# Four MLPs on one core: the place of a few inner-activation tiles in the on-chip memory

## The chip, the cores and the metric

One core of a Trainium2 chip runs the whole program in one launch. The metric is the device time of that launch in microseconds; the kernel before takes 1617.34 us (median of three runs, 1616.33 to 1620.15).

## What is computed

An encoder of four layers over one sequence of 256 tokens with 1024 channels, all in fp32. A layer is a mixer and an MLP, each added to the residual x. The mixers are a bidirectional state-space mixer (layers 0 and 3), a dilated attention (layer 1) and a differential attention (layer 2). The change is in the MLP:

```
def sqrelu_mlp(h, w1, w2):                  # w1: 1024 x 4096, w2: 4096 x 1024
    return jnp.square(jax.nn.relu(h @ w1)) @ w2
x = x + sqrelu_mlp(rmsnorm(x, norm_mlp_g[i]), mlp_w1[i], mlp_w2[i])
```

## The kernel before, in words

All activations stand transposed: 128 channels of a block on the partitions, the 256 tokens along a row. A product in fp32 is made of three matmuls in the type float32r (`mm3`, L145 to L151): the weight's rounded part times the activation's rounded part (L149), the same weight times the activation's remainder (L150), and the weight's remainder times the activation's rounded part (L151). In `mm3` the weights are the stationary operand (`lhsT`, 128x128, 512 bytes of each partition) and the activations the moving one (`rhs`, 128x256, 1024 bytes of each partition), so every matmul has its own weight load.

**Weights.** They come as chunks of 512 KB into `raw` tiles (SyncE's queue, five buffers); ScalarE copies each to `whi` (L110), VectorE makes `wlo` (L112), five buffers of each. `pump` keeps a fixed number of chunks converted ahead of their use and of transfers ahead of the conversion.

**One MLP** (`mlp`) has eight slices s of 512 inner channels. `up(s)` takes 4 chunks and makes 96 matmuls: 8 blocks of the normalised input (the tiles `spl`) by 4 blocks of inner channels by 3. `evac(s, b)` makes relu, the norm's factor and the square on VectorE and ScalarE (L349, L351), then the rounded part `hh` and the remainder `hl` (L353, L354), in two halves of two row blocks each; a tile holds four row blocks j of 128 inner channels. `down(s)` takes 4 chunks, one for each j, and makes 96 matmuls: 4 row blocks by 8 output blocks by 3. The order is `up(0)`, `up(1)`, `down(0)`, `up(2)`, `down(1)`, ... `up(7)`, `down(6)`, `down(7)`. In the first MLP alone, `bias_vectors` (its matmuls are L721 and L722) stands between `up(2)` and `down(1)`, and `bias_rows` (transfers only) between `up(3)` and `down(2)`. The last `down` finishes the output blocks one by one (`proj_tail`), and the next part's squares and split tiles follow behind each.

**Places.** The built program gives each tile a fixed address in a partition. The weight tiles begin at 52,512 bytes and are 4096 bytes long, all of them at 288 modulo 512. The tiles `spl`, `hh`, `hl`, and the mixers' `nh` and `nl` all begin at 480 modulo 512, so that each moving operand of these lies 192 bytes past the weights' offset. Weight columns and tokens are stepped by whole multiples of 512 bytes, so the offset is the same for every matmul of a pair of tiles. Other pairs differ: in the differential attention the moving keys `k` and `kl` and the stationary queries `q` (`mm2`, L130 and L131) all begin at 0 modulo 512, a distance of 0; in the dilated attention `k` of L149 to L151 lies at a distance of 480 from `q` for part of the heads; `oh` and `tab` of L721 and L722 both lie at 480, a distance of 0. The pool `lp` of one part (an MLP or a mixer) is given back at its end, and the next part's pool begins at the same address, 127,456.

Of the kernel before, what the change touches and what calls it, by code (L numbers as in the profile page):

```python
# [10 lines left out]
F32 = mybir.dt.float32  # L11
F32R = mybir.dt.float32r
I32 = mybir.dt.int32
AF = mybir.ActivationFunctionType
ALU = mybir.AluOpType
PSUM = bass.MemoryType.PSUM
P = 128
T = 256
# [27 lines left out]
class Prog:  # L46
# [278 lines left out]
    def mlp(self, l, finish):  # L325
        nc = self.nc
        hs = {}
        acc = [self.bank(f"a{i}") for i in range(4)]

        def up(s):  # L330
            b = [self.bank(f"r{2 * (s % 2) + i}") for i in range(2)]
            for j in range(4):
                wh, wl = self.take(("up", l, s, j))
                for kk in range(2):
                    k = 2 * j + kk
                    for n in range(4):
                        c = slice(kk * 512 + n * P, kk * 512 + (n + 1) * P)
                        self.mm3(b[n // 2][:, (n % 2) * T:(n % 2 + 1) * T], wh[:, c], wl[:, c],
                                 self.uh[k], self.ul[k], k == 0 and n % 2 == 0, k == 7)
                self.done()  # L340
            return b

        def evac(s, b):
            hh = self.lp.tile([P, 4, T], F32R, tag="hh", name="hh", bufs=2)
            hl = self.lp.tile([P, 4, T], F32R, tag="hl", name="hl", bufs=2)
            for i in range(2):
                v = self.lp.tile([P, 2, T], F32, tag="v", name="v", bufs=3)
                sq = self.lp.tile([P, 2, T], F32, tag="vsq", name="vsq", bufs=2)
                nc.vector.scalar_tensor_tensor(out=v, in0=b[i].rearrange("p (n t) -> p n t", n=2), scalar=0.0,  # L349
                                               in1=self.rbc.unsqueeze(1).to_broadcast([P, 2, T]), op0=ALU.max, op1=ALU.mult)  # L350
                nc.scalar.activation(out=sq, in_=v, func=AF.Square)  # L351
                h = hh[:, 2 * i:2 * i + 2, :]
                nc.scalar.copy(out=h, in_=sq)  # L353
                nc.vector.tensor_tensor(out=hl[:, 2 * i:2 * i + 2, :], in0=sq, in1=h.bitcast(F32), op=ALU.subtract)  # L354
            hs[s] = (hh, hl)

        def down(s):
            hh, hl = hs.pop(s)
            if s < 7:
                for j in range(4):  # L360
                    wh, wl = self.take(("dn", l, s, j))
                    for n in range(8):
                        c = slice(n * P, (n + 1) * P)
                        self.mm3(acc[n % 4][:, (n // 4) * T:(n // 4 + 1) * T], wh[:, c], wl[:, c], hh[:, j, :], hl[:, j, :],
                                 s == 0 and j == 0 and n < 4, False)
                    self.done()
            else:
                self.proj_tail(acc, ("dn", l), [(hh[:, j, :], hl[:, j, :]) for j in range(4)], finish)

        b = up(0)  # L370
        self.norm_finish("a3")
        evac(0, b)
        for s in range(1, 8):
            b = up(s)
            evac(s, b)
            if s == 2 and not self.bvec:
                self.bias_vectors()
            if s == 3 and not self.rep:
                self.bias_rows()
            down(s - 1)  # L380
        down(7)

    def tail_chunks(self, key, w, k0, nk):
# [888 lines left out]
```

## Time and profile before

| what | us |
|---|---|
| median of three runs | 1617.34 |
| the profiled execution | 1616.8 |
| span of its trace (first to last instruction) | 1615.0 |
| TensorE (PE) busy | 1579.2 (98%) |
| VectorE (DVE) busy | 1193.0 (74%) |
| ScalarE (ACT) busy | 959.2 (59%) |
| transfers (DMA), mean | 186 GB/s |

The MLPs lie at about 262 to 432, 731 to 902, 1030 to 1197 and 1436 to 1607 us of the span. How to read the rows further on: a matmul's duration (0.28 us) covers its way through the pipeline, and the next one starts long before it ends; the pace is the distance from one start to the next. A row of a window counts the matmuls that touch it, some two or three more than begin in it.

### The profile page before, as it was taken

What the parts mean: (1) busy time and instruction counts of PE and PEld (TensorE: products, weight loads), DVE (VectorE), ACT (ScalarE), POOL (GpSimd) and SP (SyncE); (2) the same over time, 40 slices, a digit from 0 to 9 for tenths busy, and PEclk for the clock granted to TensorE, in tenths of its full rate; (3) what the DMA queues carried; (4) which work ended last, traced back from release to release, by engine and by line L of the source; (5) the groups of instructions that cost most, each with busy time, mean ns of one, the idle gap of its engine ahead of it and who ended that gap; (6) DMA issues with size and microseconds to landing.
All of it is one profiled execution on the core that took longest, in us unless ns stands there. A gap on an engine that the chain in (4) does not pass through costs nothing.

```text
span 1615.0 us, 32385 instructions
## 1 busy us (share of the span) xinstructions
PE 1579.2 (98%) x13018; PEld 1534.2 (95%) x13018; DVE 1193.0 (74%) x1996; ACT 959.2 (59%) x1627; POOL 133.1 (8%) x122
## 2 busy tenths in 40 slices
PE   8999999999999999999999999999999999999998
PEld 7989899999989999999999999999998898899997
DVE  6999998555776667666555899755578999985554
ACT  5577866444566666764444677644455777664444
POOL 0012131000200000010000100100010231310001
PEclk9999999999999999999999999999999999999999
DMA  6677765665565555546566575566656677656661
GB/s 210 216 217 235 218 198 177 214 212 188 150 172 166 166 158 168 161 132 200 184 186 190 157 216 151 173 197 191 191 161 183 211 219 226 214 176 190 193 194 65
DMA packets 230294, 299.84 MB, mean 186 GB/s; under 512 B 16496, under 2 KB 166256, under 8 KB 230144
## 3 DMA queue, kind: packets, MB, share of 16 engines
q1 hardware_dynamic: 209552, 262.51, 53.1%
q10 hardware_dynamic: 20592, 35.27, 7.6%
q8 instruction: 102, 1.67, 0.4%
q14 instruction: 48, 0.39, 0.1%
HBM read 296.41 MB, written 3.62 MB: 186 GB/s over the span
## 4 chain that ended last, share of the span: by engine, by line
PE 75%; DVE 13%; DMA 5%; ACT 3%; issue 2%; POOL 0%; SPq 0%; DVEq 0%; ACTq 0%; POOLq 0%
PE r L149 13%; PE r L151 13%; PE r L150 13%; PE a L149 8%; PE a L150 8%; PE a L151 8%; DVE wlo L112 3%; DMA raw<-in_ssd_in_w_dram 2%; PE r L147 2%; DMA bc<-scr 1%; PE a L829 1%; PE a L830 1%; PE a L828 1%; PE r L620 1%; ACT whi L110 1%
## 5 line engine op out<-in xcount | busy, mean ns | idle before, releaser
L112 DVE TENSOR_TENSOR wlo<-raw,whi 128x1024 fp32r<-128x1024 f32 (+1 forms) x490 | 591.3, 1214 | 301.6 <-ACT whi L110 299.9
L110 ACT CAST whi<-raw 128x1024 fp32r<-128x1024 f32 (+1 forms) x490 | 503.1, 1034 | 450.6 <-PE r L150 224.4
L151 PE MATMUL r<-spl,wlo 128*128 128x256 f32 x1248 | 352.1, 282 | 3.7 <-DVE wlo L112 3.7
L149 PE MATMUL r<-spl,whi 128*128 128x256 f32 x1248 | 353.5, 283 | 0.5 <-ACT whi L110 0.5
L150 PE MATMUL r<-spl,whi 128*128 128x256 f32 x1248 | 353.2, 283 | 0.4
L149 PE MATMUL r<-nh,whi 128*128 128x256 f32 (+1 forms) x1024 | 291.6, 285 | 6.7 <-DVE kl L142 3.2
L151 PE MATMUL r<-nh,wlo 128*128 128x256 f32 (+1 forms) x1024 | 286.9, 280 | 2.2 <-DVE wlo L112 2.2
L150 PE MATMUL r<-nl,whi 128*128 128x256 f32 (+1 forms) x1024 | 286.8, 280 | 0.0
L150 PE MATMUL a<-hl,whi 128*128 128x256 f32 x1024 | 286.0, 279 | 0.0
L149 PE MATMUL a<-hh,whi 128*128 128x256 f32 x1024 | 286.0, 279 | 0.0
L151 PE MATMUL a<-hh,wlo 128*128 128x256 f32 x1024 | 285.6, 279 | 0.0
L151 PEld LDWEIGHTS r<-spl,wlo 128*128 128x128 f32 x1248 | 238.5, 191 | 4.3 <-DVE wlo L112 4.1
L150 PEld LDWEIGHTS r<-spl,whi 128*128 128x128 f32 x1248 | 239.1, 192 | 1.3 <-DVE spl L233 1.1
L149 PEld LDWEIGHTS r<-spl,whi 128*128 128x128 f32 x1248 | 238.7, 191 | 1.1 <-ACT whi L110 0.7
L149 PEld LDWEIGHTS r<-nh,whi 128*128 128x128 f32 (+1 forms) x1024 | 193.4, 189 | 11.0 <-issue 6.1
L151 PEld LDWEIGHTS r<-nh,wlo 128*128 128x128 f32 (+1 forms) x1024 | 193.3, 189 | 3.2 <-DVE wlo L112 2.4
L150 PEld LDWEIGHTS r<-nl,whi 128*128 128x128 f32 (+1 forms) x1024 | 193.8, 189 | 0.7 <-DVE nl L306 0.2
L149 PEld LDWEIGHTS a<-hh,whi 128*128 128x128 f32 x1024 | 193.4, 189 | 0.2 <-ACT whi L110 0.2
L150 PEld LDWEIGHTS a<-hl,whi 128*128 128x128 f32 x1024 | 193.5, 189 | 0.0
L151 PEld LDWEIGHTS a<-hh,wlo 128*128 128x128 f32 x1024 | 192.4, 188 | 0.0
L246 POOL TENSOR_TENSOR sqacc<-sqacc,sq 128x256 f32<-128x256 f32 x48 | 43.3, 901 | 1100.8 <-ACT sq L244 1099.1
L595 ACT ACTIVATE e<-bc,tb 128x256 f32<-128x256 f32 (+1 forms) x256 | 95.5, 446 | 1.5 <-issue 1.5
(249 smaller groups left out, 2400.8 us busy)
## 6 DMA issues: line engine op xcount, KB each, us to landing
raw<-in_mlp_w_dram SPq DMA_DIRECT2D x256, 512.0 KB
raw<-in_ssd_in_w_dram SPq DMA_DIRECT2D x96, 512.0 KB
bc<-scr ACTq DMA_DIRECT2D x32, 768.0 KB
raw<-in_dil_qkv_w_dram SPq DMA_DIRECT2D x48, 512.0 KB
raw<-in_ssd_out_w_dram SPq DMA_DIRECT2D x32, 512.0 KB
raw<-in_dil_qkv_w_dram SPq DMA_DIRECT2D x64, 192.0 KB
raw<-in_diff_qkv_w_dram SPq DMA_DIRECT2D x24, 512.0 KB
raw<-in_dil_out_w_dram SPq DMA_DIRECT2D x8, 512.0 KB
```

What stands on the lines that cost most here:

```text
L110: self.nc.scalar.copy(out=hi[:, :n], in_=raw[:, :n])
L112: self.nc.vector.tensor_tensor(out=lo[:, :n], in0=raw[:, :n], in1=hi[:, :n].bitcast(F32), op=ALU.subtract)
L147: mm(out, lhsT=wh, rhs=xh, start=start, stop=stop, skip_group_check=True)
L149: mm(out, lhsT=wh, rhs=xh, start=start, stop=False, skip_group_check=True)
L150: mm(out, lhsT=wh, rhs=xl, start=False, stop=False, skip_group_check=True)
L151: mm(out, lhsT=wl, rhs=xh, start=False, stop=stop, skip_group_check=True)
L246: nc.gpsimd.tensor_tensor(out=self.sqs[0], in0=self.sqs[0], in1=sq, op=ALU.add)
L595: X = lambda o, i_, bias: nc.scalar.activation(out=o, in_=i_, func=AF.Exp, bias=bias)
L620: nc.tensor.matmul(b[(h % 2) * 64:(h % 2) * 64 + 64, n * T:(n + 1) * T], lhsT=xt[:, 1 - i, h * 64:(h + 1) * 64], rhs=G[h][:, i * T:(i + 1) ...
L828: mm(o, lhsT=nh[:, k, t], rhs=w_h, start=k == 0, stop=False)
L829: mm(o, lhsT=nh[:, k, t], rhs=w_l, start=False, stop=False)
L830: mm(o, lhsT=nl[:, k, t], rhs=w_h, start=False, stop=k == 7)
```

## The change

The MLP's pool gets four new tiles ahead of the others: a pad of 320 bytes that nothing uses, the tiles `h0` and `l0` of two row blocks each, and a pad of 192 bytes. With the pad the pool's begin (127,456, at 480 modulo 512) goes to 127,776, at 288; `h0` and `l0` thus lie at a distance of 0 from the weights. The second pad brings the tiles behind it back to 480; these all move by 4,608 bytes, nine times 512. For s = 0 in each MLP, and in the first MLP for s = 4 as well (`self.rep` is still empty there), the first half of `evac` writes to `h0` and `l0` in place of the first halves of `hh` and `hl`, and `down(s)` reads its row blocks j = 0 and 1 there: 48 matmuls. The number, the order, the shapes and the types of all instructions stay as they were.

```
+        self.lp.tile([P, 80], F32, name="gap0")
+        same = [self.lp.tile([P, 2, T], F32R, name=n) for n in ("h0", "l0")]
+        self.lp.tile([P, 48], F32, name="gap1")
+        resets = (0,) if self.rep else (0, 4)
         def evac(s, b):
             hh = self.lp.tile([P, 4, T], F32R, tag="hh", name="hh", bufs=2)
             hl = self.lp.tile([P, 4, T], F32R, tag="hl", name="hl", bufs=2)
+            hs[s] = [(hh[:, j, :], hl[:, j, :]) for j in range(4)]
+            if s in resets:
+                hs[s][:2] = [(same[0][:, j, :], same[1][:, j, :]) for j in range(2)]
...
-                h = hh[:, 2 * i:2 * i + 2, :]
+                h, lo = (hh[:, 2 * i:2 * i + 2, :], hl[:, 2 * i:2 * i + 2, :]) if i or s not in resets else same
                 nc.scalar.copy(out=h, in_=sq)
-                nc.vector.tensor_tensor(out=hl[:, 2 * i:2 * i + 2, :], in0=sq, in1=h.bitcast(F32), op=ALU.subtract)
-            hs[s] = (hh, hl)
+                nc.vector.tensor_tensor(out=lo, in0=sq, in1=h.bitcast(F32), op=ALU.subtract)
         def down(s):
-            hh, hl = hs.pop(s)
+            h = hs.pop(s)
...
-                        self.mm3(acc[n % 4][:, (n // 4) * T:(n // 4 + 1) * T], wh[:, c], wl[:, c], hh[:, j, :], hl[:, j, :],
+                        self.mm3(acc[n % 4][:, (n // 4) * T:(n // 4 + 1) * T], wh[:, c], wl[:, c], *h[j],
                                  s == 0 and j == 0 and n < 4, False)
...
-                self.proj_tail(acc, ("dn", l), [(hh[:, j, :], hl[:, j, :]) for j in range(4)], finish)
+                self.proj_tail(acc, ("dn", l), h, finish)
```

## Rows read from the trace of the kernel before

**Rows 1.** The head of the profile's page: the span, and the busy time of the engines with their share of it.

```profile
span 1615.0 us, 32385 instructions
PE 1579.2 (98%) x13018; PEld 1534.2 (95%) x13018; DVE 1193.0 (74%) x1996; ACT 959.2 (59%) x1627; POOL 133.1 (8%) x122
```

**Rows 2.** The waits of TensorE, the two longest sums: the engine and line that waited, what for, us in total, times, the longest one.

```profile
PE r L151 <- DVE wlo L112: 5.8, 2, 3.7
PE a L274 <- POOL sqacc L246: 4.5, 3, 2.4
```

**Rows 3.** The windows view, one window in each MLP, in order: its bounds and length, PE's busy time and matmuls, the granted clock as a share of full speed, the share of the transfer engines, GB/s.

```profile
360.00:420.00 60.00, 60.00 (x512) 1.00 0.61 186
825.00:865.00 40.00, 40.00 (x342) 1.00 0.62 188
1060.00:1100.00 40.00, 40.00 (x356) 1.00 0.62 192
1460.00:1500.00 40.00, 40.00 (x356) 1.00 0.65 197
```

**Rows 4.** The timeline of PE, first and last row of a stretch in which every matmul has a row: the first MLP (190 rows), then the second (190 rows). The columns are the start in us, the duration, and the instruction.

```profile
345.73 0.28 PE L149 MATMUL a<-hh,whi 128*128 128x256 f32 x1
...
367.99 0.28 PE L149 MATMUL a<-hh,whi 128*128 128x256 f32 x1
...
825.73 0.28 PE L151 MATMUL r<-spl,wlo 128*128 128x256 f32 x1
...
847.99 0.28 PE L151 MATMUL r<-spl,wlo 128*128 128x256 f32 x1
```

**Rows 5.** The same for the fourth MLP (197 rows).

```profile
1459.73 0.28 PE L150 MATMUL a<-hl,whi 128*128 128x256 f32 x1
...
1481.94 0.28 PE L151 MATMUL a<-hh,wlo 128*128 128x256 f32 x1
```

**Rows 6.** The timeline of PE in the differential attention: matmuls at a distance of 192 bytes, then eight at 0 (L130, L131), then at 192 again.

```profile
928.11 0.28 PE L150 MATMUL r<-nl,whi 128*128 128x256 f32 x1
928.23 0.28 PE L151 MATMUL r<-nh,wlo 128*128 128x256 f32 x1
928.35 0.28 PE L130 MATMUL r<-k,q 128*128 128x256 f32 x1
...
928.58 0.28 PE L130 MATMUL r<-k,q 128*128 128x256 f32 x1
...
929.30 0.28 PE L149 MATMUL r<-nh,whi 128*128 128x256 f32 x1
929.42 0.29 PE L150 MATMUL r<-nl,whi 128*128 128x256 f32 x1
929.54 0.28 PE L151 MATMUL r<-nh,wlo 128*128 128x256 f32 x1
...
929.78 0.28 PE L150 MATMUL r<-nl,whi 128*128 128x256 f32 x1
...
931.14 0.28 PE L150 MATMUL r<-nl,whi 128*128 128x256 f32 x1
```

**Rows 7.** The same view further on, after the last of four matmuls at a distance of 0: the last of them, the ones at 192 behind it, and (last row) the sixth row after the fourth.

```profile
989.50 0.28 PE L131 MATMUL r<-kl,q 128*128 128x256 f32 x1
989.62 0.28 PE L151 MATMUL r<-spl,wlo 128*128 128x256 f32 x1
989.73 0.28 PE L149 MATMUL r<-spl,whi 128*128 128x256 f32 x1
989.85 0.28 PE L150 MATMUL r<-spl,whi 128*128 128x256 f32 x1
...
990.54 0.28 PE L150 MATMUL r<-spl,whi 128*128 128x256 f32 x1
```

**Rows 8.** The timeline of PE in the dilated attention: the last matmul at a distance of 480, then the first and the eighth at 192.

```profile
470.26 0.28 PE L151 MATMUL r<-k,q 128*128 128x256 f32 x1
470.38 0.28 PE L149 MATMUL r<-nh,whi 128*128 128x256 f32 x1
...
471.21 0.28 PE L150 MATMUL r<-nl,whi 128*128 128x256 f32 x1
```

**Rows 9.** The timeline of PE in the first MLP around the matmuls of `bias_vectors`, and the sixth row after the one at 294.85.

```profile
293.21 1.03 PE L721 MATMUL r<-oh,tab 32*16 32x512 f32 x2
294.08 0.38 PE L722 MATMUL r<-oh,tab 32*16 32x128 f32 x2
294.38 0.39 PE L149 MATMUL a<-hh,whi 128*128 128x256 f32 x1
...
294.85 0.28 PE L149 MATMUL a<-hh,whi 128*128 128x256 f32 x1
...
295.56 0.28 PE L149 MATMUL a<-hh,whi 128*128 128x256 f32 x1
```

**Rows 10.** The windows view behind the first MLP (three windows), the second and the third; columns as in rows 3.

```profile
435.00:440.00 5.00, 4.36 (x20) 0.52 0.35 97
440.00:445.00 5.00, 5.00 (x36) 0.79 0.50 137
460.00:465.00 5.00, 5.00 (x35) 1.00 1.07 267
905.00:910.00 5.00, 4.77 (x28) 0.66 0.66 210
1200.00:1205.00 5.00, 5.00 (x30) 0.68 0.38 110
```

## The prediction, made before the changed kernel ran

> **What bounds the kernel.** The page's head comes first: TensorE (PE) is busy for 1579.2 of 1615.0 us, the next engine for 74% [rows 1]. The view of waits comes second: the longest sum that PE waits for any one releaser is 5.8 us in the whole run [rows 2]. So inside the MLPs the time is the number of matmuls times their pace, and a change that adds and removes no instruction can only act through the pace. The windows come third, and here is what the reader is to see: four windows, one in each MLP, PE busy throughout and the granted clock at 1.00 (the level of 2.4 GHz) in all, and yet 342 matmuls in 40 us of the second MLP against 356 in the third and fourth [rows 3]. The same instructions run at two paces. The timeline gives them: 22.26 us over 189 steps in the first and in the second MLP is **117.8 ns** a matmul [rows 4], 22.21 us over 196 steps in the fourth is **113.3 ns** [rows 5]. I call them the slow and the fast pace; a step is 4.5 ns. Whichever pace an MLP has, the window shows it held for tens of microseconds; nothing but a disturbance of the stream changes it. Transfers don't decide: their share is 0.61 and 0.62 at the slow pace, 0.62 and 0.65 at the fast one [rows 3].
>
> **Does a stretch at distance 0 change the pace?** That is what the edit would do, and the differential attention holds the experiment in small. In rows 6 the stream comes in at the slow pace, one step of 0.12 us; then eight matmuls at distance 0 take over without a break, and the last six of them take 929.30 - 928.58 = 0.72 us, **120 ns** each; behind them, at 192 again, come steps of 0.12, 0.12 and two in 0.24, and then 1.36 us for 12 steps from 929.78 on: 113.3 ns [rows 6]. Slow in, distance 0, fast out, within four or five matmuls. In rows 7 four at distance 0 are followed by two steps of 0.11 and 0.12 and then 0.69 us for six: 115 ns over the six, the first of them still long, the rest fast [rows 7]. Against it stands a case at distance 480, not 0: behind it seven steps take 0.83 us, 118.6 ns, the slow pace [rows 8]. So 0 and 480 differ, as the edit wants.
>
> The Trainium skill speaks against the edit: "TensorE: Matmul & The Clock Gate", section "Step-by-step: what each phase is for", says that TensorE has two independent read ports, one for the streaming operand and one for weight loads, so that loading the next weights takes nothing from the running matmul. By that rule the distance of the two operands could not matter and the sum would be zero. The trace disagrees as far as 113.3, 117.8 and 120 ns for matmuls of one shape and one clock go; no row shows the ports themselves.
>
> **The change part by part.**
>
> *Instructions, transfers, queues.* None is added, removed or moved, on SP's and POOL's queues neither. The writes of `evac` go to another address with the same shapes; I cost them at nothing, and what hides them is the 96 matmuls of the next `up` that stand between `evac(s)` and `down(s)`, 10.9 us at 113.3 ns. If that cover went, PE would wait for ScalarE's and VectorE's copies, but the cover is not touched. The tiles behind the pads move by 4,608 bytes and lie over other tiles of the parts before and after; all their users are done by then, since PE finishes an MLP before the next norm starts; zero.
>
> *The blocks at distance 0.* Each is 48 matmuls at 120 ns [rows 6]. In a slow stream that costs 48 x 2.2 = 0.11 us, in a fast one 48 x 6.7 = 0.32. First MLP two blocks in a slow stream, 0.21; second MLP one, 0.11; third and fourth, both fast already [rows 3], 0.64 together. Sum **+0.96 us**. Ends: 113.3 ns (nothing) and 122 (the longest step that I would read out of 0.12) for five blocks, 0 to 1.6 us.
>
> *Second MLP, slow before.* 1536 matmuls, 8 x 192. Before the block's end lie `up(0)`, `up(1)` and 48: 240. The other 1296 go from 117.8 to 113.3: **-5.83 us**. Nothing disturbs this MLP on its way, as the third and fourth keep the fast pace all through.
>
> *First MLP, slow before.* Behind the first block 48 + 96 matmuls (rest of `down(0)`, `up(2)`) come fast: -0.65. Then `bias_vectors` breaks the stream: four fp32 matmuls, 1.2 us, after which the stream before was slow, 0.71 us for six steps [rows 9]. Unknown: whether the break throws a fast stream back. Ends: it keeps what it finds (the 576 matmuls from `down(1)` to `up(5)` gain 2.6 us) or it sets slow (they gain nothing). I take slow: the break drains PE, the same four matmuls and the same first weight load follow, and slow is what the trace shows behind them. Then the second block, at `down(4)`; 528 matmuls are left behind it: -2.38. Sum for this MLP **-3.03 us**.
>
> *Third and fourth MLP.* Fast before; the block ends fast again by rows 6 and 7. Their cost is in the blocks.
>
> *What is late next.* At the fast pace the third and fourth MLP show no idle PE with the same weights' traffic [rows 3], so the gain isn't caught inside. Behind each MLP PE waits for the norm and restarts at a granted clock of 0.52, 0.66 and 0.68 in a 5 us window, partly the level of 1.2 GHz [rows 10]. These stretches move with the MLP's end. How long the low clock lasts may move with the shift: 20 matmuls in 5 us against 44 at full pace. Bounds: 2.5 us either way for one such window; I take zero.
>
> **Sum.** 0.96 - 5.83 - 3.03 = -7.9 us. The profiled execution has 1616.8 us: a span of 1615.0 and 1.8 around it. 1616.8 - 7.9 = **1608.9 us**. The median of the runs is 0.5 above the profiled one, so against it I'd be at a gain of 0.5%. A difference of 0.2% (3.2 us) is about what a measurement of this kernel can tell from none.
>
> **The rivals.**
>
> *The break keeps the fast pace.* 2.6 us more gained in the first MLP, and its second block costs 0.32 in place of 0.11: 1616.8 - 10.3 = **1606.5 us**. For it: rows 9 have a slow stream ahead of the break as well, so they don't say what a fast one would do. Against: the drain. Chance 0.16.
>
> *The gain is given back behind the MLPs.* The dilated attention starts with transfers that fill their engines (share 1.07 [rows 10]); if these can't move up, or the low clock lasts longer by one window, 2.5 to 5 us come back: **1612 to 1614 us**. Against: transfers are held by buffers that come free as PE goes on, and would move up with it. Chance 0.10.
>
> *Nothing switches.* Either the place doesn't matter, as the skill's rule has it, or the pace behind 48 matmuls is the one ahead of them, as behind the block at distance 480 [rows 8]. The first gives **1616.8**, the second only the blocks' cost, **1617.8 us**. For it: the weights in rows 6 are of another kind and the block is of 8, not 48; against it: slow in, fast out, twice without a break. Chance 0.13.
>
> *Slower: distance 0 sets the slow pace.* Place: the rest of `down(0)` in the third and fourth MLP, both fast before. The pace hangs on where in the weight load the stream of activations stands when the block ends; if 48 matmuls drift to a point in the slow one's reach, 2 x 1296 matmuls take 4.5 ns more: +11.7, with the blocks **1629.4 us**. It decides as soon as one of these two MLPs turns (+5.8) and the second one doesn't. For it: `oh` and `tab` too lie at distance 0, and behind them the stream is slow [rows 9], though there PE was drained. Against: rows 6 and 7. Chance 0.09.
>
> **How the numbers follow.** The forecast has 0.52, with its own range of 1606 to 1612 (the low clock and the mixers' stretches, each of which has one pace or the other and may change it). Fast-end and given-back cases add 0.26; from 1604.5 to 1614.0 us the three hold 0.78, about 8 in 10. Faster by over 0.2%: the same three, 0.78; within it 0.13; slower 0.09.
>
> **What the changed profile would show.** Second MLP: a window of 40 us with 356 matmuls in place of 342, from its first `down` to its end. First MLP: fast from 276 us to `bias_vectors`, slow behind it, fast again from the second block (some 368 us) on; if fast all through, the first rival. The 48 matmuls on `h0` and `l0` at 0.12 us in all four. Third and fourth: 356 as before. PE's idle time and the engines' busy times unchanged. The prediction is wrong if the second MLP still shows 342 behind its block, or the third or fourth turns to it.

## The result, and the profile after

The changed kernel takes 1606.76 us (median of six runs, 1602.9 to 1608.06) against 1616.62 us of the kernel before on the same chip (six runs, 1613.63 to 1620.15): a ratio of 0.9936, 95% interval 0.992 to 0.9951. Three executions are left out here and below: two in which the granted clock was 0.65 and 0.56 over the whole run (2222.82 and 2606.70 us), and one of the kernel before, of 1627.26 us at a clock of 0.99, that lies over 1.5% above the fastest of its set. The profiled execution took 1607.3 us, with a span of 1605.5, 9.5 below the one before.

The head of the page after, against [rows 1]:

```profile
span 1605.5 us, 32382 instructions
PE 1570.2 (98%) x13018; PEld 1524.9 (95%) x13018; DVE 1193.4 (74%) x1996; ACT 959.3 (60%) x1627; POOL 132.4 (8%) x122
```

PE has the same 13018 matmuls and is busy 9.0 us less; the other engines have the same work. The windows view after (bounds and length, PE's busy time and matmuls, granted clock, transfers' share, GB/s): first MLP twice, then one window for each of the others, against [rows 3]:

```profile
296.00:356.00 60.00, 60.00 (x532) 1.00 0.72 228
360.00:420.00 60.00, 60.00 (x529) 1.00 0.62 193
825.00:865.00 40.00, 40.00 (x355) 1.00 0.65 197
1060.00:1100.00 40.00, 40.00 (x355) 1.00 0.64 191
1460.00:1500.00 40.00, 40.00 (x355) 1.00 0.64 193
```

All four MLPs are fast now: 355 in 40 us in the second, which had 342. The first has 529 in the window that had 512, three below the 532 of the window ahead of it since its second block lies in there. Where the second MLP turns, in the timeline of PE (start, duration, instruction; the last matmuls on `spl`, the first and the ones behind the block at distance 0):

```profile
736.39 0.28 PE L149 MATMUL r<-spl,whi 128*128 128x256 f32 x1
736.51 0.28 PE L150 MATMUL r<-spl,whi 128*128 128x256 f32 x1
736.63 0.28 PE L151 MATMUL r<-spl,wlo 128*128 128x256 f32 x1
736.75 0.28 PE L149 MATMUL a<-h,whi 128*128 128x256 f32 x1
...
742.50 0.29 PE L149 MATMUL a<-hh,whi 128*128 128x256 f32 x1
...
742.86 0.28 PE L149 MATMUL a<-hh,whi 128*128 128x256 f32 x1
...
743.20 0.28 PE L149 MATMUL a<-hh,whi 128*128 128x256 f32 x1
...
744.22 0.28 PE L149 MATMUL a<-hh,whi 128*128 128x256 f32 x1
```

Steps of 0.12 come in; the block's 48 steps take 742.50 - 736.75 = 5.75 us, 119.8 ns each; three steps of 0.12 follow, and from 743.20 on nine take 1.02 us, 113.3 ns. And the break of `bias_vectors` in the first MLP, against [rows 9] (the same lines under new numbers), with a window ahead of it:

```profile
282.00:292.00 10.00, 10.00 (x90) 1.00 0.62 190
...
294.15 1.03 PE L729 MATMUL r<-oh,tab 32*16 32x512 f32 x2
295.01 0.38 PE L730 MATMUL r<-oh,tab 32*16 32x128 f32 x2
295.32 0.39 PE L149 MATMUL a<-hh,whi 128*128 128x256 f32 x1
```

The fast pace went in (90 matmuls in 10 us), and behind it the window 296 to 356 holds 532 matmuls: the fast pace came out. In the trace before, the slow pace went in and came out:

```profile
282.00:292.00 10.00, 10.00 (x87) 1.00 0.63 180
296.00:356.00 60.00, 60.00 (x512) 1.00 0.69 221
```

By stretches, from the starts of the first and the last matmul of the `down` calls of each MLP in the timelines of the two profiles:

| stretch | before, us | after, us | difference |
|---|---|---|---|
| ahead of the first MLP's first `down` | 270.50 | 271.96 | +1.46 |
| first MLP, `down(0)` to `down(7)` | 159.56 | 154.25 | -5.31 |
| to the second MLP's | 312.05 | 310.53 | -1.52 |
| second MLP | 158.18 | 152.54 | -5.64 |
| to the third MLP's | 141.21 | 143.42 | +2.21 |
| third MLP | 152.21 | 152.55 | +0.34 |
| to the fourth MLP's | 257.43 | 255.99 | -1.44 |
| fourth MLP | 154.49 | 154.89 | +0.40 |

The MLPs together give -10.2 us; the stretches between them, which the change doesn't touch, move by up to 2.2 us each way and by 0.7 in sum.

### The profile page after: what moved, and what is told of

It is laid out like the page before. It is cut to its first block, busy times and chain, and to the rows that moved or that the text cites. A ratio compares the mean times of both kernels' runs of the same rounds, so it can differ in the third digit from the quotient of the medians.

```text
span 1605.5 us, 32382 instructions
## 1 busy us (share of the span) xinstructions
PE 1570.2 (98%) x13018; PEld 1524.9 (95%) x13018; DVE 1193.4 (74%) x1996; ACT 959.3 (60%) x1627; POOL 132.4 (8%) x122
## 4 chain that ended last, share of the span: by engine, by line
PE 79%; DVE 12%; ACT 3%; DMA 3%; issue 2%; POOL 1%; SPq 0%; DVEq 0%; ACTq 0%; POOLq 0%
PE r L149 14%; PE r L151 14%; PE r L150 13%; PE a L149 8%; PE a L151 8%; PE a L150 8%; DVE wlo L112 4%; PE r L147 2%; DMA raw<-in_ssd_in_w_dram 2%; PE r L628 1%; PE a L836 1%; PE a L838 1%; PE a L837 1%; DVE spl L233 1%; PE a L895 1%
## 5 line engine op out<-in xcount | busy, mean ns | idle before, releaser
L149 PE MATMUL a<-hh,whi 128*128 128x256 f32 x944 | 261.0, 277 | 0.0
L150 PE MATMUL a<-hl,whi 128*128 128x256 f32 x944 | 260.9, 276 | 0.0
L151 PE MATMUL a<-hh,wlo 128*128 128x256 f32 x944 | 260.4, 276 | 0.0
L149 PEld LDWEIGHTS a<-hh,whi 128*128 128x128 f32 x944 | 177.2, 188 | 0.2 <-ACT whi L110 0.2
L150 PEld LDWEIGHTS a<-hl,whi 128*128 128x128 f32 x944 | 177.2, 188 | 0.0
L151 PEld LDWEIGHTS a<-hh,wlo 128*128 128x128 f32 x944 | 177.2, 188 | 0.0
```

The lines of the kernel that those rows point to most:

```text
L149: mm(out, lhsT=wh, rhs=xh, start=start, stop=False, skip_group_check=True)
L150: mm(out, lhsT=wh, rhs=xl, start=False, stop=False, skip_group_check=True)
L151: mm(out, lhsT=wl, rhs=xh, start=False, stop=stop, skip_group_check=True)
```

## The experiments

Theory: the distance of the moving operand from the stationary one, modulo some power of two, decides; a stretch at distance 0 leaves the stream at the fast pace whatever came in, and at 192 a stream holds the pace that it has. Rivals: the separate tiles or the shift by 4,608 bytes act; any change of tile acts; the slow pace belongs to certain MLPs.

**The same tiles at distance 192** (`e1_place192`).

```
-        self.lp.tile([P, 80], F32, name="gap0")
+        self.lp.tile([P, 128], F32, name="gap0")
         same = [self.lp.tile([P, 2, T], F32R, name=n) for n in ("h0", "l0")]
-        self.lp.tile([P, 48], F32, name="gap1")
```

> The same tiles h0 and l0, the same slices, the same shift of 4,608 bytes for all that lies behind, but the pad of 320 bytes is 512 and the second one is gone: h0 and l0 lie at a distance of 192, not 0. If the distance is what acts: no block at 120 ns; each MLP keeps the pace that it enters with, so its down(1) to down(6) show 117.8 ns where it enters slow; where the first two MLPs enter slow and the others fast, as before, 1616.6 us, ratio to before 1.000. If the separate tiles or the shift act: the four MLPs go fast at down(0) as in the changed kernel, ratio 0.994, some 1607 us.

Measured: 1612.69 us (ten runs, 1608.22 to 1624.04) against 1613.0 (19 runs, 1602.23 to 1625.99), ratio 1.0014, 0.998 to 1.0047. The windows view, one line for each MLP:

```profile
360.00:420.00 60.00, 60.00 (x532) 1.00 0.65 195
825.00:865.00 40.00, 40.00 (x342) 1.00 0.60 191
1060.00:1100.00 40.00, 40.00 (x355) 1.00 0.63 190
1460.00:1500.00 40.00, 40.00 (x355) 1.00 0.65 196
```

The second MLP stays slow through to its end with the separate tiles and the shift in place. So these don't act, the distance does. The first MLP shows what the expectation had left open: it is fast with no block at all, where it was slow in the first profile.

**No second block in the first MLP** (`e2_first_only`, again as `e8_first_again`).

```
-        resets = (0,) if self.rep else (0, 4)
+        resets = (0,)
```

> The block at distance 0 in the first slice only, in the first MLP too; the second one there (slice 4) is gone. If the break of bias_vectors keeps the pace that it finds: the first MLP is fast from the block to its end, and is shorter than the changed kernel's by 48 x 6.7 ns = 0.3 us (from the first matmul on h0 to the last down: 153.9 against 154.25 us). If the break throws the stream back to the slow pace in some executions or always: the first MLP is slow from down(1) to its end, 1104 + 48 matmuls at 4.5 ns more, 5.2 us longer (159.4 us).

> The block at distance 0 in the first slice of each MLP alone, beside the changed kernel on one chip. If the break of bias_vectors keeps what it finds: 0.3 us less than the changed kernel, no difference that the runs can tell (ratio of the two 0.999 to 1.001), and the first MLP fast in the trace to its end. If the break throws some executions back: now and then a run 5 us longer.

Measured: 1604.8 us (ten runs, 1602.12 to 1609.43; ratio to before 0.9961, 0.9931 to 0.999), and on another chip 1607.57 (eleven runs, 1603.34 to 1610.61; 0.9935, 0.9908 to 0.9961), beside 1606.73 for the changed kernel there: no difference that the runs can tell. In both profiles the first MLP's `down` calls take 153.92 us, as the first theory had it to the tenth. Of the first profile, the windows behind the break and where the second block was:

```profile
296.00:356.00 60.00, 60.00 (x532) 1.00 0.72 227
360.00:420.00 60.00, 60.00 (x532) 1.00 0.63 194
```

The break kept the fast pace that it found; the second block was not needed in these executions.

**A map of distances** (`e3_map`): one pair of tiles for each of the slices 0 to 6, pads between them.

```
+        dist = {0: (480, 0, 480, 64, 448, 128, 384), 1: (384, 0, 256, 320, 96, 416, 160),
+                2: (32, 352, 224, 288, 0, 64, 128), 3: (448, 320, 256, 96, 160, 416, 32)}[l]
+        resets = range(7)
```

> In each MLP, slices 0 to 6 have their first two row blocks in tiles of their own at one distance each: first MLP 480, 0, 480, 64, 448, 128, 384; second 384, 0, 256, 320, 96, 416, 160; third 32, 352, 224, 288, 0, 64, 128; fourth 448, 320, 256, 96, 160, 416, 32. Each block is 48 matmuls, with 144 at 192 behind it. If the distance decides the pace: each distance has one steady pace inside its block whenever it comes (0: 120 ns), and behind it leaves one pace, whatever came in (0: fast); 480 leaves slow or what it found. If only the break of the pattern acts (any other distance does it): all blocks leave the fast pace. If the place does nothing by itself: paces inside blocks don't repeat from one MLP to the next.

Measured: 1609.17 us (one run). Pace inside the block (last 24 of its 48 steps, from the timeline), and the pace ahead and behind:

| distance | in the block, ns | ahead, behind (times seen) |
|---|---|---|
| 0, 256 | 120.0, 120.0 | fast, fast (3 and 1); 256 also slow, fast (1) |
| 32, 288 | 116.7, 116.7 | fast, fast (2 and 1) |
| 64, 320 | 117.8, 117.8 | fast, fast (2 and 1); 320 also slow, slow (1) |
| 96, 352 | 120.0, 120.0 | fast, fast (2 and 1) |
| 128, 384 | 118.8, 118.8 | fast, fast (2 and 2) |
| 160, 416 | 117.4, 117.4 | fast, fast (2 and 2) |
| 192, 448 | 113.3 or 117.8 | held; 448 both ways (1 and 1) |
| 224, 480 | 118.4, 118.3 | fast, fast (1 and 2) |

Each pair 256 apart agrees within 0.1 ns, in different MLPs and slices: at the distances tested, in steps of 32 bytes, the period is 256 bytes, not 512. Only the fourth MLP came in slow. Its windows: within the block at 448 and behind it, the same for 320, the same for 256:

```profile
1441.00:1446.00 5.00, 5.00 (x45) 1.00 0.65 213
1448.00:1461.00 13.00, 13.00 (x113) 1.00 0.60 182
1464.00:1468.00 4.00, 4.00 (x37) 1.00 0.68 231
1470.00:1484.00 14.00, 14.00 (x121) 1.00 0.62 189
1487.00:1491.00 4.00, 4.00 (x36) 1.00 0.59 213
1493.00:1507.00 14.00, 14.00 (x126) 1.00 0.65 194
```

Two of the matmuls counted in each line began ahead of its window, so 121 and 126 in the same 14 us are the slow and the fast pace. The block at 448, by the period the same place as 192, and the block at 320 left the slow pace alone; 256 ended it. So neither a change of tile (448) nor every change of distance (320) is enough, and 0 and 256 act alike. The other distances were only met by a fast stream here; whether they too would turn a slow one stays open (the short stretch at 480 in [rows 8] left one slow).

One rival the map can't rule out by itself: the weights lie at the same place in all its blocks, so the moving tile's own place modulo 256 could act in place of the distance. The differential attention speaks against it. Its `k` and `kl` begin at 0 modulo 512, a place that with the MLPs' weights would be a distance of 224 and 118.4 ns; with `q` at 0 too, the last six steps of the block in [rows 6] take 0.72 us, and so do those of the blocks at 948.87 and 970.82 us of that trace: 120 ns each, as at distance 0 in the map, where 118.4 would make 0.71 us.

**How short a block is enough** (`e4_dose`, then `e5_dose_own`).

```
+        dose = {0: 1, 1: 2, 2: 3, 3: 4, 4: 6, 5: 8}
+                if i == 0 and s in dose:
+                    nc.scalar.copy(out=same[0], in_=sq[:, 0, :])
+                    nc.vector.tensor_tensor(out=same[1], in0=sq[:, 0, :], in1=same[0].bitcast(F32), op=ALU.subtract)
...
-                        ... *h[j],
+                        ... *(same if j == 0 and n < dose.get(s, 0) else h[j]),
```

> How short a block at distance 0 is enough. Row block j = 0 is written twice, once more at distance 0 (two small copies on ScalarE and VectorE for each slice); down(s) reads that copy in its first n output blocks, 3n matmuls: 3, 6, 9, 12, 18, 24 for slices 0 to 5. In a stream that enters slow (as all four MLPs did in the changed kernel's trace): if it is a drift towards a point, a few matmuls leave it slow and some number turns it; by the differential attention's rows, where 4 and 8 were enough, the turn comes with 3 or 6. If the number has to be near 48, the pace stays slow until a late slice. An MLP that enters fast stays fast throughout.

One pair of tiles served all slices in the first form, and the next slice's copy is written ahead of the read, so the blocks read the next slice's values and PE waited for them: 1634.73 us. Most blocks were also issued in two pieces, with matmuls at 192 between. So this form doesn't answer its question, but what it shows bears on the theory. The third MLP's first slice, with three matmuls at 0 as one and two, then the first MLP's second slice, with six as two and four:

```profile
1046.90 0.28 PE L149 MATMUL a<-hh,whi 128*128 128x256 f32 x1
...
1047.24 0.28 PE L149 MATMUL a<-hh,whi 128*128 128x256 f32 x1
1047.58 0.39 PE L149 MATMUL a<-h,whi 128*128 128x256 f32 x1
...
1048.67 0.28 PE L149 MATMUL a<-hh,whi 128*128 128x256 f32 x1
...
1050.09 0.28 PE L149 MATMUL a<-hh,whi 128*128 128x256 f32 x1
```

```profile
294.17 0.28 PE L151 MATMUL a<-hh,wlo 128*128 128x256 f32 x1
...
295.30 0.28 PE L149 MATMUL a<-hh,whi 128*128 128x256 f32 x1
295.41 0.39 PE L149 MATMUL a<-h,whi 128*128 128x256 f32 x2
...
296.48 0.28 PE L151 MATMUL a<-h,wlo 128*128 128x256 f32 x1
296.59 0.28 PE L149 MATMUL a<-hh,whi 128*128 128x256 f32 x1
...
298.01 0.28 PE L149 MATMUL a<-hh,whi 128*128 128x256 f32 x1
```

In the third MLP a fast stream (three steps in 0.34 us) was broken by a wait ahead of the block, and behind the block 12 steps take 1.42 us, 118 ns, until the next slice. In the first MLP a fast stream (ten steps in 1.13 us) met no wait at all, and behind the block 12 steps take 1.42 us again. The timeline gives, over the four MLPs:

- behind three in two pieces, the one stream at 117.8 ns stayed there, and of three at 113.3 ns one came out at 117.8;
- behind six in two pieces, two streams went from 117.8 to 113.3 ns and two from 113.3 to 117.8;
- behind nine and more, all came out at 113.3 ns.

So the expectation that a fast stream stays fast fell, and short pieces at distance 0 with matmuls at 192 between can leave either pace. What decides, the waits, the pieces or something else, wasn't separated; the wait alone it isn't, by the first MLP. The second form has a pair for each slice:

```
+        dose = ({0: 2, 1: 3, 2: 5, 3: 8}, {0: 1, 1: 2, 2: 4, 3: 8}, {0: 1, 1: 3, 2: 4, 3: 8}, {0: 1, 1: 2, 2: 3, 3: 8})[l]
+        same = [[self.lp.tile([P, T], F32R, name=f"{n}{s}") for n in ("h", "l")] for s in dose]
```

> How short a block at distance 0 is enough, with copies of their own for each slice, so that nothing waits (the dose before had one pair of tiles for all slices, whose next writing the block had to wait for and which was overwritten before it was read). The first row block of the slice, first n output blocks, 3n matmuls: first MLP 6, 9, 15, 24 for slices 0 to 3; second 3, 6, 12, 24; third 3, 9, 12, 24; fourth 3, 6, 9, 24. In an MLP that enters slow: by the differential attention's rows the slow pace ends behind 6 or 9, perhaps behind 3; if only a long block turns it, behind 24 or not at all. An MLP that enters fast (some will) stays fast and tells nothing but that short blocks don't turn a fast stream slow.

Measured: 1604.45 us (one run); the first three MLPs came in slow. The timeline of PE in the second, three matmuls at distance 0:

```profile
734.37 0.28 PE L149 MATMUL r<-spl,whi 128*128 128x256 f32 x1
...
734.72 0.28 PE L149 MATMUL a<-h,whi 128*128 128x256 f32 x1
734.84 0.28 PE L150 MATMUL a<-l,whi 128*128 128x256 f32 x1
734.96 0.28 PE L151 MATMUL a<-h,wlo 128*128 128x256 f32 x1
735.08 0.29 PE L149 MATMUL a<-hh,whi 128*128 128x256 f32 x1
...
735.56 0.28 PE L150 MATMUL a<-hl,whi 128*128 128x256 f32 x1
...
736.92 0.28 PE L150 MATMUL a<-hl,whi 128*128 128x256 f32 x1
```

Three steps in 0.35 us ahead (117 ns), three matmuls at 0, and 12 steps in 1.36 us from 735.56 on: 113.3 ns. The third MLP turned behind three as well, the first behind six. None of the blocks behind those turned a fast stream slow, nor did three in the fourth MLP, which came in fast. Here the matmuls of a block stood in a row (but for the first of one block of 15).

**The same in two mixers** (`e6_mixers`): on top of the first block alone, the first of the eight input blocks of the dilated and the differential attention at distance 0.

```
+            self.lp.tile([P, 80], F32, name="gap0")
+            one = [self.lp.tile([P, T], F32R, name=n) for n in ("nh0", "nl0")]
+            self.lp.tile([P, 48], F32, name="gap1")
+            nh, nl = ([o] + [t[:, k, :] for k in range(KD - 1)] for o, t in zip(one, [self.lp.tile([P, KD - 1, T], F32R, name=n) for n in ("nh", "nl")]))
```

> The block at distance 0 in slice 0 of each MLP, and in the dilated and the differential attention the first of the eight input blocks (the tiles nh and nl) at distance 0 too, so that each projection begins with 6 or 3 matmuls there. In these two mixers the matmuls at distance 192 were above 113.3 ns by 2.6 and 1.5 us in sum in the changed kernel's trace. If short blocks turn the pace: those sums fall to 1 us or less each, and the first matmuls of each projection cost up to 0.04 us, some 1 to 1.5 us in all: between 1 us slower and 2 us faster than the kernel with first blocks alone (1604.8 to 1606.8 us). If a break decides the pace anew behind each projection and the block can't: nothing but the cost, 1 to 1.5 us slower.

Measured: 1608.62 us (12 runs), beside 1606.73 for the changed kernel (12) and 1607.57 for the first block alone (11), a difference that the runs can't tell from none. The surplus over 113.3 ns, summed in the timeline over the steps between neighbouring matmuls on `spl`, `nh` and `nl` (those up to 0.13 us), is about 3.4 and 0.9 us in the two mixers, against 2.7 and 0.9 with the first block alone on the same chip: nothing gained. The first mixer's sum didn't fall to 1 us as expected, and the second's was below it already. What ended the gain, the breaks behind each projection or the short stretches in some other way, wasn't separated.

**Chance or place: the kernel before, twice more** (`e10_before_again`, `e11_before_third`), and the changed kernel again (`e7_after_again`, `e12_after_third`).

> The kernel before, once more in full, for the pace with which each MLP enters. If the entry is chance and held to the MLP's end: each MLP takes from its first matmul on hh to its last either about 153.6, 152.2, 152.2, 154.5 us (fast) or 5.9 us more, not the same ones as in the first profile, and the span is about 1603 us and 5.9 for each slow one. If the entry belongs to the MLP: slow, slow, fast, fast and 1615 us again.

> The same once more, with the same expectations; two profiles that differ in the slow MLPs show chance.

> The changed kernel beside the others of this call on one chip. If the pace with which an MLP enters is chance and the block ends the chance: its runs spread over some 6 us, those of the kernel before over more than 15 us on the same chip; its median 1605 to 1608.

> The changed kernel beside the one with three matmuls, on one chip. All four MLPs fast from their blocks on, runs from 1602 to 1608.5 us whatever the kernel before does on this chip (its runs 1602 to 1627).

The windows of the two profiles of the kernel before, one line for each MLP:

```profile
360.00:400.00 40.00, 40.00 (x356) 1.00 0.61 190
825.00:865.00 40.00, 40.00 (x342) 1.00 0.61 191
1060.00:1100.00 40.00, 40.00 (x355) 1.00 0.64 196
1460.00:1500.00 40.00, 40.00 (x355) 1.00 0.63 196
```

```profile
360.00:400.00 40.00, 40.00 (x355) 1.00 0.62 197
825.00:865.00 40.00, 40.00 (x355) 1.00 0.64 196
1060.00:1100.00 40.00, 40.00 (x355) 1.00 0.64 196
1460.00:1500.00 40.00, 40.00 (x342) 1.00 0.60 184
```

Fast, slow, fast, fast; then fast, fast, fast, slow; and slow, slow, fast, fast in the first profile [rows 3]: one program, three patterns. The fourth MLP takes 160.16 us when slow against 154.49. The pace of entry is drawn anew in each execution, and it lasts for the MLP. The spans are 1606.2 and 1606.9 us with one slow MLP, 1615.0 with two; the expected 1603 and 5.9 for each gives 1608.9 and 1614.8, so the stretches between move by 2 to 3 us besides. In the other direction the changed kernel: all MLPs fast from their blocks on in each of its three profiles, 1606.73 us against 1620.01 before on one chip (0.9922, 0.9899 to 0.9946) and 1606.02 against 1611.58 on another (0.9974, 0.9951 to 0.9997). Over the three later sets of runs the kernel before ranges from 1601.8 to 1626.0 us (1625.6 and 1624.5 the highest in the last two), the changed one, in those two, from 1601.85 to 1610.47.

Counted over all profiles, by the pace ahead of the first `down` and the time from `down(0)` to `down(7)`: with 192 throughout (three of the kernel before, one of e1) five MLPs came in slow, and all five stayed slow to their end. With a block of 48 in the first slice (three of the changed kernel, e2, e8, e6) 13 came in slow, and all 13 left the block fast. None of the 22 that came in fast, 11 of each kind, turned slow. How often an MLP comes in slow isn't the same everywhere: ten of 16 in the four profiles on the chip where the kernel before takes 1620.01 us, seven of 32 in the eight on the two where it takes 1613.0 and 1611.58.

**Three matmuls in place of 48** (`e9_three`).

```
+        dose = {0: 1}
```

> Three matmuls at distance 0 in slice 0 of each MLP (first row block, first output block), read from copies of one row block, in place of 48. If three are enough, as behind the slow entries of the second and third MLP in the run with copies of their own: all four MLPs are fast from there on, down(0) to down(7) 153.9, 152.5, 152.5 and 154.8 us, and the runs lie as low as the changed kernel's (ratio of the two 0.998 to 1.001: 1 us at most is saved, 5 x 48 dearer matmuls by 2.2 to 6.7 ns). If three turn some streams only: some MLP stays slow, 5.8 us longer each, and the runs spread further up than the changed kernel's.

Measured: 1604.21 us (12 runs, 1601.07 to 1609.58) against 1611.58, ratio 0.9949, 0.9922 to 0.9976; the changed kernel beside it 1606.02 (0.9974). The `down` calls of its four MLPs take 153.62, 152.23, 152.23 and 154.55 us, 0.6 less than with 48 in the first, which had two blocks, 0.3 less in each of the others, and within 0.1 of the kernel before's where the pace was fast. In that profile all four MLPs came in fast, so that it is the profile of the dose above that shows three turning a stream, two slow streams of two. The runs fit it: they spread over 8.5 us, as against 6.8 for the changed kernel and 22.7 for the kernel before beside them. The two ratios' intervals overlap: 1.5 us of blocks' cost saved is read off the traces, not off the runs.

## Why the prediction was right, and which step was not

The time, 1606.76 us, is 2.1 below the forecast and inside its range; the direction and the place were right. Part of the hit is luck: the forecast starts from one execution with two slow MLPs, and the medians of that set happened to lie as far apart (9.9 us) as its two profiles (9.5); in the two later sets the same change gained 13.3 and 5.6 us. By its steps:

- *Two paces, and distance 0 ends the slow one.* Right, by e1 (same tiles, other distance: nothing), e3 (256 turns, 448 and 320 hold) and e5. The rule of the Trainium skill that was weighed against it ("TensorE: Matmul & The Clock Gate", "Step-by-step: what each phase is for") is that TensorE has two independent read ports, so that a weight load takes no read bandwidth from the running matmul. As the prediction read it, the place could not matter, and e3 differs: there the place alone takes matmuls of one shape from 113.3 to 120.0 ns. No run here shows the ports, or what the place acts on. The step has a limit: it holds for matmuls in a row, not for the short pieces of e4.
- *The rival "distance 0 sets the slow pace".* It didn't come with blocks of 48 in a row, none of which left a slow stream. Its picture, a place in the weight load at which the stream stands when a block ends, no run tests; e4's three fast streams that came out slow show that a short block at distance 0 can do what it feared.
- *The blocks, 0.96 us, with ends of 0 and 1.6.* The sum is right; the ends are not. Three blocks in a slow stream and two in a fast one give -0.6 us at 113.3 ns and 1.4 at 122.
- *Second MLP, -5.83 and 0.11 for the block.* -5.64 in the table: right.
- *Third and fourth, 0.32 each.* 0.34 and 0.40: right as a sum, but not on the path that the prediction had. They came in slow this time, which lies in the stretch ahead of their first `down`, and the block turned them; a fourth MLP that stays slow takes 5.7 us more.
- *First MLP, -3.03 and 0.21.* Wrong: -5.31. The step that failed is the one named unknown, whether "the break throws a fast stream back": the sum took it to set the slow pace, and it didn't. I took slow because the trace showed slow behind it; that trace had slow ahead of it as well. The break keeps what it finds, as far as seen: fast to fast (113.3 ns over the 32 steps before and behind) in ten profiles, slow to slow (117.8) in the one where a slow stream came to it, the first. The last break ahead of each MLP, two matmuls of the norm (on `dg`), is of another kind: of 38 streams that came to it at 113.3 ns 12 left it at 117.8, and of 18 that came at 117.8 seven left it at 113.3. A break that drew like that would hardly have kept ten of ten. The slow side rests on one profile. The rival that had this said 1606.5 us, near the time that came.
- *The gain isn't given back behind the MLPs.* Right in sum. The low clock did move: behind the first MLP the ten microseconds that hold it have a mean clock of 0.83 (430 to 440) where it was 0.66 (434 to 444), behind the second 0.66 (893 to 903) for 0.83 (902 to 912). One got shorter and one longer.
- *What the prediction didn't ask.* It took first and second slow, third and fourth fast as the kernel's nature, from one profile. It is chance. The gain of an execution is 5.3 to 5.6 us for each MLP that would have stayed slow, less 0.3 to 0.6 for each that was fast anyway; with two of four slow in the profile it came out near 10 us. The kernel before is as fast as the changed one in its luckiest runs, 1601.8 to 1602.5 us on three chips, and up to 24 us slower in its others. What the change removes is that spread, and the median follows: 0.9922 to 0.9974 of the kernel before in three sets of runs.

What stays open: why there are two paces at 192, what draws the entry (it shows within some four matmuls behind the last break ahead of the MLP) and why one chip draws slow more often, what a short block in pieces leaves, and why the mixers' short blocks gained nothing.

## What to carry to other kernels

Where PE is busy throughout and one shape of matmul shows two paces in different stretches at the same granted clock, count matmuls per window before anything else, and take several profiles of the unchanged kernel: a pace that is drawn anew in each execution looks like a property of a stage in any single one. The place of the moving operand against the stationary one can be worth 6% of the pace, and a few matmuls at another place can set a state that lasts for 1,000. Try a handful in a row where a long stream begins, in tiles that nothing waits for, and look in the timeline at which state they leave: in pieces they left the wrong one too.

## What the runs showed of the hardware that was not expected

- The pace of a float32r matmul of 256 columns with its own weight load depends on the places of the two operands with a period of 256 bytes (e3, which moved the moving one in steps of 32): 113.3 ns at best (192), 116.7 to 120.0 elsewhere, all at a granted clock of 1.00.
- At 192 two paces stand side by side, 113.3 and 117.8 ns, each held over a thousand matmuls (16 MLPs of 16 without a block kept theirs); at 64 there is one pace, 117.8, and yet the stream remembers: slow ahead is slow behind, fast is fast.
- The four fp32 matmuls of `bias_vectors`, 1.2 us, don't erase that memory, in eleven profiles of eleven without a block right behind it (113.3 ns on both sides in ten, 117.8 in one).
